# RWKV blocks of a transformer kernel: 128x128 block-diagonal matrices against compact 64x64 ones

## The chip, the cores and the metric

One core of a Trainium2 chip runs the whole program in one launch. The metric is device time in microseconds (us) of that launch; lower is better. The inputs are 512 tokens of width 1024 in float32, and the weights come from HBM as a stream of 857 blocks of 128x512.

## The reference, cut to what matters

The program is a chain of layers: a SwiGLU block, a mixing layer, a second SwiGLU, then pooling, dilated attention, sparse attention and convolution layers. Only the mixing layer is touched. Half of it is an RWKV-7 recurrence over 8 heads of width 64, the other half differential attention:

```python
def rwkv7_scan(r, w, k, v, a, b):     # state S: value x key, per head
    def step(S, inp):
        r_t, w_t, k_t, v_t, a_t, b_t = inp
        sa = einsum('bhij,bhj->bhi', S, a_t)
        S = S * w_t + sa[..., None] * b_t + v_t[..., None] * k_t
        y = einsum('bhij,bhj->bhi', S, r_t)
        return S, y
...
y = (y - mu) * rsqrt(var + GN_EPS)            # per token and head
y = y * gn_w + gn_b + sum(r * k * r_k) * v
return y * gate
```

The kernel computes the recurrence in chunks of 64 tokens. Inside a chunk the effect of `sa` on later tokens is a unit triangular 64x64 matrix, which has to be inverted per head and chunk; between chunks a 64x64 state per head is carried on.

## The kernel before, in words

**Matmuls.** Weights and activations of the large matmuls are split into a high and a low part, and each product is three matmuls of 128 columns of weights and 512 moving columns (`mm3`, lines 594 to 596). A generator (`gemm_fg`, `gemm_tg`) yields after such a product, so that other work can be put between them; I call this a work step. The blocks of the recurrence are plain float32 matmuls, which the chip runs as two instructions each (two passes); a transpose is one.

**The mixing layer** (`mix_heads`). The heads are handled in four pairs (`hp`), two heads of 64 on the 128 partitions. For each pair there is a projection (`proj`), a preparation (`prep`, `rwkv_pair`: decay, normalised keys, transposes of keys and values), and two units (`rwkv_unit`), one for each half of the tokens. A unit has four groups: 2 heads by 2 blocks of 128 tokens; a block holds two chunks, so its matrices are 128x128 with two 64x64 blocks on the diagonal and zeros elsewhere. These zeros are set once (`MEMSET`).

The steps of a unit, by the name of the PSUM tile they write:

- A (L1198): 16 matmuls of 64x64 weights and 128 moving columns, then eight masks on VectorE (L1205) into X1, X2
- T (L1212): transposes of Z
- W (L1220) and TW (L1228), at five levels m = 2 to 32: the inverse Z and its transpose T are merged from blocks of m to blocks of 2m. After each of the first four, Z is made from T by four transposes (L1233) and a copy on ScalarE. At 32 the line is L1237
- pta, akv, PQ (L1242, L1248, L1253), 128x128
- E (L1259), M (L1268) and G (L1273, L1274) for each chunk
- S (L1286): the state from chunk to chunk, two matmuls and one VectorE instruction each; the second half waits for the first (`"chain" in sh`)
- Y (L1297, L1298, L1301): the output, from X1, X2 and the state, summed in PSUM
- the norm, then yT and gate (L1319, L1324, L1325).

**The order.** `fill(steps, filler, n)` takes n steps of `filler` after each step of `steps`. Here `steps` are the two units taken in turn, and `filler` is `work`, a chain of projections, preparations, attention and output rows, with `PACE = 1.0`. The preparation of the first pair runs ahead of it without filler. A planner turns this order into one queue for each engine and may move an instruction ahead of another that isn't ready; the queues are then fixed and each runs in order. PSUM gives this stretch 2 banks for large matmuls, 3 (`aux`) for the units, 2 for preparation and attention, and 1 for the attention's output. The weight stream holds 4 raw and 7 split blocks of 512 columns.

Of the kernel before, what the change touches and what calls it, by code (L numbers as in the profile page):

```python
# [48 lines left out]
PACE = 1.0  # L49
LAG = 7  # L50
# [19 lines left out]
MEMSET = 8  # L70
# [252 lines left out]
def consts():  # L323
# [6 lines left out]
    c["mz0"] = f((i[None, :] == i[:, None] + 1) & (i[None, :] % 2 == 1))  # L330
    for m in (2, 4, 8, 16, 32):
        row, col = i[:, None], i[None, :]
        c[f"lv{m}"] = f((row // (2 * m) == col // (2 * m)) & (row % (2 * m) >= m) & (col % (2 * m) < m))
# [180 lines left out]
class Build:  # L514
# [464 lines left out]
    def mix_heads(self, u, yd, yr, pm, xd):  # L979
# [50 lines left out]
        def prep(hp):  # L1030

            yield from self.rwkv_pair(hp, pairs[hp], lor, lw, pm, c, sh[hp])
# [10 lines left out]

        self.after(MEMSET, lambda: [nc.gpsimd.memset(ub[:, :2048], 0.0) for ub in ubs])
# [21 lines left out]
        def units(half):  # L1066
            for _ in range(half * LAG):
                yield
            for hp in range(4):
                while not sh[hp]:  # L1070
                    yield
                yield from self.rwkv_unit(hp, half, sh[hp], sgd, pm, c, ubs[half])
                sh[hp]["done"] = sh[hp].get("done", 0) + 1
# [13 lines left out]
        for _ in prep(0):  # L1087
            pass

        def wait_for(hp):  # L1090
            while sh[hp].get("done", 0) < 2:
                yield

        work = chain(
            proj(1),
# [6 lines left out]
        fill(interleaved([units(0), units(1)]), work, PACE)  # L1102
# [4 lines left out]
    def rwkv_pair(self, hp, tiles, lor, lw, pr, c, sh):  # L1107
# [6 lines left out]
        gup = tile_("gup", (P, 2, P), 2)  # L1114
# [46 lines left out]
        for j, (nm, src) in enumerate((("bt", eb), ("kt", ec), ("vt", v))):  # L1161
            yield
            pt = self.faux(f"pt_{nm}{hp}")
            for b in range(4):
                nc.tensor.transpose(pt[:, b * P : (b + 1) * P], src[:, b * P : (b + 1) * P], self.ident)
            tok[nm] = tile_(nm, (P, 4, P))
            self.copy(j, tok[nm].rearrange("p a b -> p (a b)"), pt)
# [8 lines left out]
    def rwkv_unit(self, hp, half, sh, sgd, pr, c, ub):  # L1176
        gup = sh["gup"]
        ar, bt, kt, tok, bv, dc, st, yr = (sh[k] for k in ("ar", "bt", "kt", "tok", "bv", "dc", "st", "y"))
# [3 lines left out]
        id = f"{hp}_{half}"  # L1182
        tile_ = lambda tag, shape, bufs=2: pr.tile(list(shape), F32, tag=f"ru_{tag}", name=f"ru_{tag}{id}", bufs=bufs)
        g4 = lambda a, n: a.rearrange("p (g n) -> p g n", n=n)
        X1, X2 = g4(ub[:, :1024], 256), g4(ub[:, 1024:2048], 256)
        Tm, Z, RH, PQ = (g4(ub[:, a : a + 512], 128) for a in (2048, 2560, 3072, 3584))
        groups = [(g, 2 * half + g // 2, g % 2) for g in range(4)]
        tk = lambda p: slice(p * P, (p + 1) * P)
        hd = lambda h: slice(64 * h, 64 * h + 64)

        ck = lambda p, q: slice(p * P + 64 * q, p * P + 64 * q + 64)
        yield
        ps = [self.aux(f"A{id}_{h}") for h in range(2)]
        for j, src in enumerate((bt, kt)):
            for x in range(2):
                for g, p, h in groups:
                    q, a = h ^ x, 256 * j + P * (g // 2)
                    mm(ps[h][hd(q), a : a + P], src[hd(h), ck(p, q)], ar[hd(h), :, ck(p, q)], start=True, stop=True)  # L1198
        for j, X in enumerate((X1, X2)):
            for h in range(2):  # L1200
                for q in range(2):
                    src = ps[h][hd(q), 256 * j : 256 * j + 256].rearrange("p (g s n) -> p g s n", s=2, n=64)
                    dst = X[hd(q), h::2].rearrange("p g (s n) -> p g s n", s=2)[:, :, :, hd(q)]
                    m2 = c["m2"][hd(q)].rearrange("p (s n) -> p s n", s=2).unsqueeze(1).to_broadcast([64, 2, 2, 64])
                    V.tensor_tensor(dst, src, m2, op=ALU.mult)  # L1205

        V.tensor_tensor(Z, X1[:, :, :P], c["mz0"].unsqueeze(1).to_broadcast([P, 4, P]), op=ALU.mult)
        V.tensor_tensor(Z, Z, self.ident.unsqueeze(1).to_broadcast([P, 4, P]), op=ALU.add)
        yield
        ps = self.aux(f"T0{id}")  # L1210
        for g in range(4):
            nc.tensor.transpose(ps[:, tk(g)], Z[:, g], self.ident)  # L1212
        S.copy(Tm, g4(ps, P))
        W = RH
        halves = lambda a, m: a.rearrange("p g (b two m) -> p g two b m", two=2, m=m)
        for m in (2, 4, 8, 16, 32):
            yield
            ps = self.aux(f"W{id}_{m}")
            for g in range(4):
                mm(ps[:, tk(g)], X1[:, g, :P], Tm[:, g], start=True, stop=True)  # L1220
            V.tensor_tensor(W, g4(ps, P), c[f"lv{m}"].unsqueeze(1).to_broadcast([P, 4, P]), op=ALU.mult)
            yield
            ps = self.aux(f"TW{id}_{m}")
            out = ps.rearrange("p (x g b m) -> p x g b m", x=2, g=4, m=m)
            left, right = halves(Tm, m)[:, :, 0], halves(Z, m)[:, :, 1]
            if m < 32:
                for g in range(4):
                    mm(out[:, 0, g], Z[:, g], halves(W, m)[:, g, 0], start=True, stop=True)  # L1228
                V.tensor_tensor(left, left, out[:, 0], op=ALU.add)
                yield  # L1230
                ps = self.aux(f"Z{id}_{m}")
                for g in range(4):
                    nc.tensor.transpose(ps[:, tk(g)], Tm[:, g], self.ident)  # L1233
                S.copy(Z, g4(ps, P))
            else:
                for g in range(4):
                    mm(out[:, 1, g], W[:, g], right[:, g], start=True, stop=True)  # L1237
                V.tensor_tensor(right, right, out[:, 1], op=ALU.add)
        yield
        pa = self.aux(f"pta{id}", 256)  # L1240
        for q in range(2):
            nc.tensor.transpose(pa[:, tk(q)], ar[:, 0, tk(2 * half + q)], self.ident)  # L1242
        S.copy(RH[:, :, :64], g4(pa, 64))
        bt_, kt_, vt_ = tok["bt"], tok["kt"], tok["vt"]
        yield
        ps = self.aux(f"akv{id}", 256)
        for g, p, h in groups:
            mm(ps[:, g * 64 : (g + 1) * 64], X2[:, g, :P], vt_[:, p, hd(h)], start=True, stop=True)  # L1248
        S.copy(RH[:, :, 64:], g4(ps, 64))
        yield  # L1250
        ps = self.aux(f"PQ{id}")
        for g, p, h in groups:
            mm(ps[:, tk(g)], Z[:, g], RH[:, g], start=True, stop=True)  # L1253
        S.copy(PQ, g4(ps, P))

        yield
        ps = self.aux(f"E{id}", 256)
        for g, p, h in groups:
            mm(ps[hd(h), tk(g // 2)], PQ[:, g, :64], X1[:, g, P:], start=True, stop=True)  # L1259
        E = RH[:, :2].rearrange("p a b -> p (a b)")  # L1260
        V.tensor_tensor(E, ps, ar[:, 1, half * 256 : (half + 1) * 256], op=ALU.add)
        M = RH[:, 2:].rearrange("p a (q n) -> p a q n", q=2)
        Gs = Tm[:, :2].rearrange("p a (q n) -> p a q n", q=2)
        for q in range(2):
            yield
            ps = self.aux(f"M{id}_{q}", 128)
            for g, p, h in groups:
                mm(ps[hd(h), hd(g // 2)], PQ[hd(q), g, :64], bt_[hd(q), p, hd(h)], start=True, stop=True)  # L1268
            V.tensor_tensor(M[:, :, q], g4(ps, 64), c["i64"].unsqueeze(1).to_broadcast([P, 2, 64]), op=ALU.add)
            yield  # L1270
            ps = self.aux(f"G{id}_{q}", 128)
            for g, p, h in groups:
                mm(ps[hd(h), hd(g // 2)], bt_[hd(q), p, hd(h)], PQ[hd(q), g, 64:], start=True, stop=False)  # L1273
                mm(ps[hd(h), hd(g // 2)], kt_[hd(q), p, hd(h)], vt_[hd(q), p, hd(h)], start=False, stop=True)  # L1274
            dcq = dc[:, 4 * half + q : 4 * half + q + 3 : 2]
            V.tensor_tensor(Gs[:, :, q], g4(ps, 64), dcq.unsqueeze(2).to_broadcast([P, 2, 64]), op=ALU.mult)
        while half and "chain" not in sh:
            yield
        for cc in range(4):
            ch = 4 * half + cc  # L1280
            if ch == 7:
                break
            yield
            ps = self.aux(f"S{id}_{cc}", 64)
            for h in range(2):
                mm(ps[hd(h)], M[hd(h), cc // 2, cc % 2], st[hd(h), ch], start=True, stop=True)  # L1286
# [938 lines left out]
```

## Time and profile before

| | |
|---|---|
| median of 3 runs | 2875.74 us (2873.99 to 2876.14) |
| the profiled execution | 2876.86 us |
| its span, first to last instruction | 2875.0 us |
| TensorE matmul busy | 2816.1 us, 98% of the span |
| VectorE, ScalarE busy | 1544.8 us (54%), 1194.8 us (42%) |
| the units of the recurrence | from about 443 to 839 us |

PE is TensorE's matmul queue, PEld its weight loads, DVE VectorE, ACT ScalarE, POOL GpSimd, SP the queue that issues DMAs. A matmul's duration in a row runs to its modelled end, and the next one starts before that; what a matmul costs is read from start to start.

### The profile page before, as it was taken

The page shows a single profiled execution, that of the slowest core. Times are in us where ns is not written, and L with a number is a line of the kernel's source. Part 1 is how long each engine was busy: PE and PEld are TensorE (multiplying, and loading weights), DVE is VectorE, ACT ScalarE, POOL GpSimd, SP SyncE. Part 2 cuts the span into 40 slices and gives each one's busy share as a digit, 9 for nine tenths or more (in the row PEclk, how much of TensorE's full clock was granted, in tenths as well). Part 3 has the DMA queues.
Part 4 walks back from the last instruction along what each step waited for, and adds up shares of the span by engine and source line. Part 5 has one row for each costly group of instructions (what it writes and reads, how often), then busy time and mean ns, then how long its engine had stood idle before and what let it go on. Part 6 is the DMA issues. An engine that isn't in the chain of part 4 may idle for free.

```text
span 2875.0 us, 44121 instructions
## 1 busy us (share of the span) xinstructions
PE 2816.1 (98%) x16743; PEld 2390.0 (83%) x16743; DVE 1544.8 (54%) x3349; ACT 1194.8 (42%) x2504; POOL 430.6 (15%) x509
## 2 busy tenths in 40 slices
PE   8999999999999999999999999999999999999998
PEld 7888887868878888888888888889999787888887
DVE  5443276565666443255445533444566995577732
ACT  5333253233334333343333444444455646554431
POOL 2110041010014110011312200011004023200001
PEclk9999999999999999999999999999999999999999
DMA  4333351101122333333232332222232412133332
GB/s 142 96 99 96 99 164 37 41 21 41 34 71 79 100 96 96 103 96 96 88 107 81 89 104 78 89 84 76 77 93 81 107 59 67 61 104 97 96 95 74
DMA packets 136140, 245.30 MB, mean 85 GB/s; under 512 B 15064, under 2 KB 22232, under 8 KB 135800
## 3 DMA queue, kind: packets, MB, share of 16 engines
q1 hardware_dynamic: 135928, 242.49, 28.1%
q8 instruction: 131, 2.15, 0.3%
q14 instruction: 81, 0.66, 0.1%
HBM read 235.75 MB, written 6.68 MB: 84 GB/s over the span
## 4 chain that ended last, share of the span: by engine, by line
PE 87%; DVE 6%; ACT 2%; POOL 2%; issue 1%; DMA 1%; SPq 0%; POOLq 0%; DVEq 0%; ACTq 0%
PE f_gu L594 5%; PE f_gu L596 5%; PE f_gu L595 5%; PE kq L594 3%; PE kq L595 3%; PE kq L596 3%; PE cf L596 3%; PE cf L595 3%; PE cf L594 3%; PE f L594 3%; PE f L595 3%; PE f L596 3%; PE dO L1606 2%; PE v L594 2%; PE v L596 2%; PE v L595 2%
## 5 line engine op out<-in xcount | busy, mean ns | idle before, releaser
L184 DVE TENSOR_TENSOR wlo<-wraw,whi 128x512 fp32r<-128x512 f32 (+1 forms) x858 | 625.8, 734 | 698.7 <-ACT whi L183 697.3
L183 ACT CAST whi<-wraw 128x512 fp32r<-128x512 f32 (+1 forms) x858 | 528.4, 619 | 917.9 <-PE f_gu L596 275.0
L594 PE MATMUL f<-f_ah,wlo 128*128 128x512 f32 (+1 forms) x440 | 153.7, 349 | 1.1 <-DVE wlo L184 1.1
L596 PE MATMUL f<-f_ah,whi 128*128 128x512 f32 (+1 forms) x440 | 153.3, 348 | 0.0
L595 PE MATMUL f<-f_al,whi 128*128 128x512 f32 (+1 forms) x440 | 153.2, 348 | 0.0
L594 PE MATMUL f_gu<-n_uh,wlo 128*128 128x512 f32 (+1 forms) x376 | 142.8, 381 | 8.3 <-ACT n_uh L788 7.3
L594 PE MATMUL f_gu<-won_uh,wlo 128*128 128x512 f32 (+1 forms) x376 | 142.7, 379 | 0.0
L595 PE MATMUL f_gu<-n_ul,whi 128*128 128x512 f32 (+1 forms) x376 | 142.5, 379 | 0.0
L596 PE MATMUL f_gu<-won_uh,whi 128*128 128x512 f32 (+1 forms) x376 | 142.5, 379 | 0.0
L596 PE MATMUL f_gu<-n_uh,whi 128*128 128x512 f32 (+1 forms) x376 | 142.3, 379 | 0.0
L595 PE MATMUL f_gu<-won_ul,whi 128*128 128x512 f32 (+1 forms) x376 | 142.1, 378 | 0.0
L594 PE MATMUL cf<-w3on_uh,wlo 128*128 128x512 f32 (+1 forms) x376 | 141.5, 376 | 0.0
L595 PE MATMUL cf<-w3on_ul,whi 128*128 128x512 f32 (+1 forms) x376 | 141.2, 375 | 0.0
L596 PE MATMUL cf<-w3on_uh,whi 128*128 128x512 f32 (+1 forms) x376 | 141.1, 375 | 0.0
L594 PE MATMUL kq<-dl_uh,wlo 128*128 128x512 f32 x256 | 101.9, 398 | 0.0
L595 PE MATMUL kq<-dl_ul,whi 128*128 128x512 f32 x256 | 100.5, 393 | 0.0
L1576 ACT ACTIVATE ds<-ds,dmx 128x128 f32<-128x128 f32 (+1 forms) x192 | 79.7, 417 | 49.8 <-DVE dmx L1575 49.8
L596 PE MATMUL kq<-dl_uh,whi 128*128 128x512 f32 x256 | 99.8, 390 | 0.0
L594 PEld LDWEIGHTS f<-f_ah,wlo 128*128 128x128 f32 x440 | 82.6, 188 | 13.4 <-DVE wlo L184 1.3
L596 PEld LDWEIGHTS f<-f_ah,whi 128*128 128x128 f32 x440 | 82.6, 188 | 12.2
L595 PEld LDWEIGHTS f<-f_al,whi 128*128 128x128 f32 x440 | 82.6, 188 | 12.1
L594 PEld LDWEIGHTS f_gu<-n_uh,wlo 128*128 128x128 f32 x376 | 71.9, 192 | 21.3 <-ACT n_uh L788 7.3
(831 smaller groups left out, 7511.3 us busy)
## 6 DMA issues: line engine op xcount, KB each, us to landing
wraw<-w SPq DMA_DIRECT2D x856, 256.0 KB, 2.6
dperm<-dnat SPq DMA_DIRECT2D x4, 528.0 KB, 3.1
dl_acc<-dperm SPq DMA_DIRECT2D x4, 528.0 KB, 3.8
x<-x SPq DMA_DIRECT2D x4, 512.0 KB, 6.1
xd<-x SPq DMA_DIRECT2D x8, 256.0 KB, 2.9
x<-xd SPq DMA_DIRECT2D x8, 256.0 KB, 3.4
toep<-rvd SPq DMA_DIRECT2D x8, 256.0 KB, 4.7
out<-x SPq DMA_DIRECT2D x16, 128.0 KB, 1.8
```

The costliest lines, as they stand in the source:

```text
L183: b.nc.scalar.copy(hi[:, s], raw[:, s])
L184: b.nc.vector.tensor_tensor(lo[:, s], raw[:, s], hi[:, s].bitcast(F32), op=ALU.subtract)
L594: mm(ps, a[1], b[0], start=start, stop=False)
L595: mm(ps, a[0], b[1], start=False, stop=False)
L596: mm(ps, a[0], b[0], start=False, stop=stop)
L1576: S.activation(o, o, AF.Exp, bias=mx[:, i, h : h + 1], scale=-1.0, accum_out=zz[:, i, h : h + 1])
L1606: mm(po[0][:, i % 2, h], pT[:, b, a + j * P : a + (j + 1) * P], vt[:, kt, h * 64 : (h + 1) * 64], start=j == 0, stop=j == nb - 1)
```

## The change

Every block of the recurrence is stored as 64x64 on 64 partitions, chunk q of a block on partitions 64q to 64q+63, so that the 128x128 matrices with their zeros go. Both halves of the tokens are handled in one unit of eight groups (4 blocks by 2 heads). `rwkv_unit` becomes `rwkv_head` (A to G, and the part of Y that needs no state, `yl`) and `rwkv_tail` (the chain S, the part of Y from the state, norm, yT, gate). The tail of a pair is stepped beside the head of the next pair. Z is no longer made from T by transposes: both are updated by matmuls. `PACE` is 3, and the first preparation takes two steps of the next pair's projection after each of its own. `gup` and two of the transposed operands keep one buffer instead of two or lie in the units' memory, and the zeroing goes.

```diff
-PACE = 1.0
-LAG = 7
+PACE = 3
...
-        self.after(MEMSET, lambda: [nc.gpsimd.memset(ub[:, :2048], 0.0) for ub in ubs])
...
+        def units():
+            tail = iter(())
             for hp in range(4):
                 while not sh[hp]:
+                    next(tail, None)
                     yield
+                for _ in self.rwkv_head(hp, sh[hp], c, at):
+                    next(tail, None)
+                    yield
+                for _ in tail:
+                    yield
+                tail = self.rwkv_tail(hp, sh[hp], sgd, pm, c, at)
+            for _ in tail:
+                yield
...
-        for _ in prep(0):
-            pass
+        first = proj(1, apart("z1"))
+        fill(prep(0), first, FIRST_PACE)
...
-        fill(interleaved([units(0), units(1)]), work, PACE)
+        fill(units(), work, PACE)
...
-        gup = tile_("gup", (P, 2, P), 2)
+        gup = tile_("gup", (P, 2, P))
...
+        groups = [(2 * p + h, p, h) for p in range(4) for h in range(2)]
+        each = [(g, p, h, q) for g, p, h in groups for q in range(2)]
+        crossed = [(2 * p + h, p, h, h ^ x) for p in range(4) for x in range(2) for h in range(2)]
...
+            for g, p, h, q in crossed:                                  # A
+                mm(ps[h][hd(q), p * P : (p + 1) * P], src[hd(h), ck(p, q)], ar[hd(h), :, ck(p, q)], start=True, stop=True)
+            for h in range(2):
+                V.tensor_tensor(X[:, h::2], g4(ps[h]), c["m2"]..., op=ALU.mult)
...
+            for g, p, h, q in each:                                     # W
+                mm(ps[hd(q), blk(g)], X1[hd(q), g, :64], Tm[hd(q), g], start=True, stop=True)
+            V.tensor_tensor(W, g8(ps), bc(c[f"lv{m}"]), op=ALU.mult)
+            yield
...
+            for g, p, h, q in each if m < 32 else ():                   # TW
+                mm(out[hd(q), 0, g], Z[hd(q), g], halves(W, m)[hd(q), g, 0], start=True, stop=True)
+            for g, p, h, q in each:
+                mm(out[hd(q), 1, g], W[hd(q), g], right[hd(q), g], start=True, stop=True)
+            if m < 32:
+                V.tensor_tensor(left, left, out[:, 0], op=ALU.add)
+            V.tensor_tensor(right, right, out[:, 1], op=ALU.add)
...
+        for g, p, h, q in crossed:                                      # E, then M
+            mm(ps[q][hd(h), blk(p)], PQ[hd(q), g, :64], X1[hd(q), g, 64:], start=True, stop=True)
...
+        ps = self.aux(f"yl{hp}")
+        for g, p, h in groups:
+            for q in range(2):
+                mm(ps[hd(q), blk(g)], X1[hd(q), g, 64:], PQ[hd(q), g, 64:], start=True, stop=False)
+            for q in range(2):
+                mm(ps[hd(q), blk(g)], X2[hd(q), g, 64:], vt_[hd(q), p, hd(h)], start=False, stop=True)
...
+        for ch in range(1, 7):                                          # S, in rwkv_tail
             for h in range(2):
+                mm(ps[hd(h)], M[hd(h), ch], st[hd(h), ch], start=True, stop=True)
+            V.scalar_tensor_tensor(st[:, ch + 1], ps, dc[:, ch : ch + 1], Gs[:, ch], op0=ALU.mult, op1=ALU.add)
             yield
+        for ch in range(8):                                             # Y
+            p, q = ch // 2, ch % 2
+            for h in range(2):
+                mm(py[h][hd(q), 64 * p : 64 * p + 64], E[hd(h), ch], st[hd(h), ch], start=True, stop=True)
```

T (16 matmuls with the 64x64 identity), akv and PQ go over `each` as W does; PQ has 128 moving columns. G goes over `crossed`, two matmuls for each entry.

## Rows read from the trace of the kernel before

**Rows 1.** Busy time in stretches: us, each engine's busy us (instructions), clock, DMA

```profile
428.00:450.00 22.00, 20.95 (x125) 15.26 (x125) 16.37 (x31) 10.81 (x17) 5.29 (x3) 0.92 0.20 61
...
656.00:840.00 184.00, 181.67 (x1418) 145.22 (x1416) 110.64 (x292) 61.57 (x129) 11.32 (x11) 1.00 0.14 43
sum 390.00, PE 381.81 PEld 303.01 DVE 235.73 ACT 132.01 POOL 28.29; mean PE 127.27 PEld 101.00 DVE 78.58 ACT 44.00 POOL 9.43
```

**Rows 2.** Chain of waits, 560 to 571 us: start us, us, piece

```profile
562.92 0.23 PE rkv L596
563.14 0.84 PE TW L1228 x8
563.99 0.44 PE Z L1233 x4
...
565.64 1.79 PE W L1220 x16
```

**Rows 3.** PE in order of time, 511 to 518 us: start, us, engine line instruction

```profile
511.31 0.40 PE L596 MATMUL dqk<-f1n_uh,whi 128*128 128x512 f32 x1
511.64 0.33 PE L1286 MATMUL S<-rw_st,ub 64*64 64x64 f32 x4
511.90 0.50 PE L594 MATMUL dqk<-f1n_uh,wlo 128*128 128x512 f32 x1
512.24 0.39 PE L595 MATMUL dqk<-f1n_ul,whi 128*128 128x512 f32 x1
...
513.97 0.33 PE L1297 MATMUL Y<-ub 128*128 128x64 f32 x2
...
515.57 0.50 PE L594 MATMUL dqk<-f1n_uh,wlo 128*128 128x512 f32 x1
...
516.47 0.34 PE L1273 MATMUL G<-x,rw_bt 64*64 64x64 f32 x4
516.63 0.29 PE L1274 MATMUL G<-rw_vt,rw_kt 64*64 64x64 f32 x4
516.75 0.33 PE L1273 MATMUL G<-x,rw_bt 64*64 64x64 f32 x4
516.87 0.33 PE L1274 MATMUL G<-rw_vt,rw_kt 64*64 64x64 f32 x4
517.13 0.50 PE L594 MATMUL dqk<-f1n_uh,wlo 128*128 128x512 f32 x1
```

**Rows 4.** PE in order of time, around an M step at 493 us

```profile
493.34 0.45 PE L1268 MATMUL M<-rw_bt,ub 64*64 64x64 f32 x8
493.72 0.50 PE L594 MATMUL dqk<-f1n_uh,wlo 128*128 128x512 f32 x1
```

**Rows 5.** PE in order of time, an A step at 531 us

```profile
530.82 0.68 PE L1198 MATMUL A<-rw_ar,rw_eb 64*64 64x128 f32 x16
531.30 0.67 PE L1198 MATMUL A<-rw_ar,k 64*64 64x128 f32 x16
531.90 0.39 PE L594 MATMUL dv<-whi,f1n_ul 128*128 128x256 f32 x1
```

**Rows 6.** PE in order of time, an E step at 585 us

```profile
584.68 0.40 PE L596 MATMUL rkv<-f1n_uh,whi 128*128 128x512 f32 x1
585.00 0.66 PE L1259 MATMUL E<-ub 128*64 128x128 f32 x8
585.59 0.60 PE L474 MATMUL d_o<-dv,d_pT 128*128 128x128 f32 x3
```

**Rows 7.** Groups by line, 400 to 860 us: busy us, mean ns | idle before

```profile
L1221 DVE TENSOR_TENSOR x<-W,cst 128x512 f32<-128x512 f32 x20 | 13.8, 690 | 18.1 <-PE W L1220 17.9
```

**Rows 8.** Waits of the DMA queue, 450 to 840 us: us in total, times, longest

```profile
SPq L1115 <- PE gate L1325: 18.3, 2, 17.4
```

**Rows 9.** PE in order of time, an A step at 551 us beside an attention score

```profile
551.52 0.43 PE L1198 MATMUL A<-rw_ar,rw_eb 64*64 64x128 f32 x2
551.88 0.48 PE L441 MATMUL d_ps<-dqk 64*128 64x128 f32 x2
```

More of the change, by code (lines that the diff above doesn't have):

```diff
@@ L1030, in prep @@
         def prep(hp):
-            yield from self.rwkv_pair(hp, pairs[hp], lor, lw, pm, c, sh[hp])
+            yield from self.rwkv_pair(hp, pairs[hp], lor, lw, pm, c, sh[hp], ubs[0])
         diff = DiffAttention(self, u, yd, pm, c)
@@ L1085, in apart @@
             return zs
-        for _ in prep(0):
-            pass
+        first = proj(1, apart("z1"))
+        fill(prep(0), first, FIRST_PACE)
         def wait_for(hp):
-            while sh[hp].get("done", 0) < 2:
+            while "done" not in sh[hp]:
                 yield
         work = chain(
-            proj(1),
+            first,
             shared(diff.project(0), prep(1), PREP_PACE),
@@ L1174, in rwkv_pair, with rwkv_places @@
         sh.update(gup=gup, ar=ar, bt=eb, kt=ec, tok=tok, bv=v, dc=dc, st=st, y=r)
-    def rwkv_unit(self, hp, half, sh, sgd, pr, c, ub):
+    def rwkv_places(self, ub):
+        lo, hi = ub
+        g8 = lambda a: a.rearrange("p (g n) -> p g n", g=8)
+        t = dict(X1=g8(lo[:, :1024]), X2=g8(lo[:, 1024:2048]), PQ=g8(lo[:, 2048:3072]))
+        for j, n in enumerate(("T", "Z", "W", "E", "M", "G", "yl", "yc")):
+            t[n] = g8(hi[:, 512 * j : 512 * (j + 1)])
+        t["R"] = hi[:, :3072].rearrange("p (a n) -> p a n", a=2)[:, :, :512].rearrange("p a (g n) -> p a g n", g=8)
+        return t
@@ L1181, in rwkv_unit @@
         mm = nc.tensor.matmul
[L1182 to L1188, printed above, removed]
@@ L1207, in rwkv_unit @@
[L1207 to L1216, printed above, removed]
-            yield
[L1218 to L1284, printed above, removed]
-            for h in range(2):
-                mm(ps[hd(h)], M[hd(h), cc // 2, cc % 2], st[hd(h), ch], start=True, stop=True)
-            V.scalar_tensor_tensor(st[:, ch + 1], ps, dc[:, ch : ch + 1], Gs[:, cc // 2, cc % 2], op0=ALU.mult, op1=ALU.add)
-        yc = Tm[:, 2:].rearrange("p a (q n) -> p (a q) n", q=2)
@@ new lines, in rwkv_tail @@
+        py = [self.aux(f"Y{hp}_{h}", 256) for h in range(2)]
+        for ch in range(8):
+            p, q = ch // 2, ch % 2
+            for h in range(2):
+                mm(py[h][hd(q), 64 * p : 64 * p + 64], E[hd(h), ch], st[hd(h), ch], start=True, stop=True)
+        for h in range(2):
+            V.tensor_tensor(yc[:, h::2], py[h].rearrange("p (g n) -> p g n", g=4), yl[:, h::2], op=ALU.add)
+        s = tile_("s", (P, 8))
+        b8 = lambda a: a.unsqueeze(2).to_broadcast([P, 8, 64])
@@ L1315, in rwkv_unit @@
+        G.tensor_tensor(rd, v2, self.mhalf[:, :1].to_broadcast([P, 8]), op=ALU.pow)
+        V.tensor_tensor(yc, yc, b8(rd), op=ALU.mult)
         for _ in range(1 + NORM_WAIT):
             yield
-        pt = self.aux(f"yT{id}", 256)
-        for q in range(2):
-            nc.tensor.transpose(pt[:, tk(q)], yc[:, 2 * q : 2 * q + 2].rearrange("p a b -> p (a b)"), self.ident)
-        cs = slice(half * 256, (half + 1) * 256)
-        t1 = Z[:, 2:].rearrange("p a b -> p (a b)")
-        V.scalar_tensor_tensor(t1, pt, self.pv("gn_w", hp), bv[:, cs], op0=ALU.mult, op1=ALU.add)
@@ L1323, in rwkv_unit @@
-        pg = self.aux(f"gate{id}", 256)
-        mm(pg, gup[:, 0], sgd[:, 0, cs], start=True, stop=False)
-        mm(pg, gup[:32, 1], sgd[:32, 1, cs], start=False, stop=True)
-        V.scalar_tensor_tensor(yr[:, cs], t1, self.pv("gn_b", hp), pg, op0=ALU.add, op1=ALU.mult)
+        pt = self.aux(f"yT{hp}")
+        for p in range(4):
+            nc.tensor.transpose(pt[:, p * P : (p + 1) * P], yc[:, 2 * p : 2 * p + 2].rearrange("p a b -> p (a b)"), self.ident)
+        t1 = yl.rearrange("p a b -> p (a b)")
@@ L1329, in ln_residual @@
+        V.scalar_tensor_tensor(t1, pt, self.pv("gn_w", hp), bv, op0=ALU.mult, op1=ALU.add)
+        pg = self.aux(f"gate{hp}")
+        mm(pg, gup[:, 0], sgd[:, 0], start=True, stop=False)
+        mm(pg, gup[:32, 1], sgd[:32, 1], start=False, stop=True)
+        V.scalar_tensor_tensor(yr, t1, self.pv("gn_b", hp), pg, op0=ALU.add, op1=ALU.mult)
+        sh["done"] = True
     def ln_residual(self, src, kt, wname, l, name, rms_g=None, ls=2):
```

139 lines of the change are left out of this document (91 added, 48 removed).

## The prediction, made before the run

> **What bounds the kernel now.** I read the busy time by stretch first, then the chain of waits, then TensorE's queue in order of time. In the stretch of the units, 450 to 840 us, PE is busy 381.8 of 390 us at full clock, VectorE 235.7 and ScalarE 132.0 [rows 1]. The chain of waits there runs from matmul to matmul [rows 2]: what ends a stretch is how long TensorE's queue is, and the 8.2 us in which it stands idle. So I price the change in TensorE time from start to start, then ask whether the new chain of steps can stall the queue, and whether another engine comes up. VectorE's load falls: one mask of W for both halves instead of two of 0.69 us [rows 7], at five levels and four pairs, is 14 us less, and the masks of A go from 16 to 4 a pair. I put these at nothing; TensorE's queue hides them.
>
> **Prices.** A large product's matmul costs 0.23 us [rows 2]. A step with 128x128 weights costs 0.11 us for each instruction: 1.79 for 16 of W, 0.84 for 8 of TW (its moving columns are half, so the weights set the price), 0.44 for 4 transposes [rows 2]. These slip in between large matmuls at no further cost.
>
> A step on 64x64 tiles is different. Its two tiles take passes side by side: in G four instructions, two passes on each tile, start every 0.12 us, so a pass costs 0.06 on its tile [rows 3]. M with four passes a tile holds the queue 0.38 us [rows 4], so 0.14 is fixed. Its neighbours pay too: S starts 0.33 after the large matmul ahead of it instead of 0.23, and the large matmul behind it holds the queue 0.34 instead of 0.23 [rows 3]. A visit to 64x64 tiles thus costs 0.14 + 0.10 + 0.11 = 0.35 us plus 0.06 for each pass of the tile that has most. G with 8 passes checks it: 0.14 + 0.48 = 0.62, measured 0.66 [rows 3]. With 128 moving columns, A: 32 instructions on four tiles, 8 passes each, 1.08 us [rows 5], (1.08 - 0.14) / 8 = 0.118 a pass.
>
> **The change, for one pair, before to after.**
> - A: two visits of 8 passes on four tiles both times. Nothing.
> - T: 8 transposes, 0.88, to 16 matmuls, 16 passes on each of two tiles, 0.35 + 0.96 = 1.31. +0.43.
> - W: five levels of 1.79 (both halves) to 1.31. -2.40.
> - TW with Z at four levels: 16 instructions of TW, 1.79, and 8 transposes, 0.88, to 32 matmuls, 32 passes a tile, 0.35 + 1.92 = 2.27. -1.60. Level 32: 1.79 to 1.31, -0.48.
> - akv: 16 instructions with 128x128 weights, 1.79, to 1.31. -0.48. PQ: 1.79 to 0.35 + 16 x 0.118 = 2.24. +0.45. pta: the same four transposes.
> - E, M, G, Y, S before: E twice 0.59 + 0.20 [rows 6]; M four times 0.38 + 0.21; G four times 0.66 + 0.21; Y four times 1.60 + 0.11 [rows 3], because it mixes both shapes; S seven times 0.26 + 0.21. That is 1.58 + 2.36 + 3.48 + 6.84 + 3.29 = 17.55. After: E and M in one visit on four tiles, 16 passes, 1.31; G on four tiles (16 passes) and yl on two (32) in one visit, 0.35 + 2.88 = 3.23; Y's part from the state on four tiles, 8 passes, 0.83; six S, which for three pairs lie next to a step of the next head and cost 0.26 each, and for the last pair 0.47: 1.88 on average. Sum 7.25. -10.30.
> - gate and yT: the same columns, half the instructions. Nothing.
>
> Together 0.43 - 2.40 - 1.60 - 0.48 - 0.48 + 0.45 - 10.30 = -14.38, times four pairs -57.5 us. Two terms aren't shown by a row of before: four tiles at 64 moving columns, and two tiles over 16 or 32 passes in a row. At the dear end a pass costs the G visit's whole 0.66 less 0.14 over 8, 0.065: with some 340 passes a pair that takes back 1.7 us, 7 us in all. At the cheap end it costs half of the 0.11 of 128 columns of weights, 0.055, and gives 7 us more. If four tiles cost what two cost twice (E, M, G, Y: 40 passes), 2.4 a pair, 10 us. I keep 0.06 and both ends for the range.
>
> **What moves.** The steps of a pair are one chain now instead of two that take turns, with three work steps between, nine matmuls, 2.05 us. A step's answer needs its last passes to drain, about 0.3 (a piece of G lasts 0.29 to 0.34 though the next one starts after 0.12 [rows 3]), and VectorE's 0.69 [rows 7], some 1.0 to 1.1; with another VectorE instruction of the same size ahead of it 1.7 to 1.8. So 2.05 covers it. What waits behind a late step is the whole queue of TensorE. In attention the work steps are lighter than a product and the cover is thinner. Counting yields, the work has about 283 steps after the first preparation. Head 0 and 1 use it up to step 102; the third preparation ends at step 142, so for 40 steps there is no head beside projection and attention; heads 2 and 3 and the last tail need 43 steps of three, to 274. So the chain ends just before the work does, and its last output isn't waited for longer than now. The three `aux` banks now serve a head and a tail; A and E/M take two banks each, G and yl all three, so a bank can be late by one VectorE instruction, 0.69. Stalls: the idle time of 8.2 us could go (-8), or 25 of the 77 head and tail steps could lack 1 us each (+25). I take +3, near the row, since the queue is planned in the same way.
>
> The first preparation gets the next pair's projection as filler. The planner has put such matmuls there already: PE is busy 20.95 of 22 us, at clock 0.92 [rows 1]. From 0 to -2; I take -1. The single `gup` makes its load wait for the gate of the pair just before; with two buffers it waited up to 17.4 us for a gate already [rows 8], and behind it on SP stand weight loads, with up to seven split blocks, 2.7 us of matmuls each, ahead. Nothing, or up to 5 us if blocks run out. Zeroing leaves POOL, 28.3 of 390 us busy [rows 1]: nothing.
>
> Sum against the profiled execution, 2876.9: -57.5 + 3 - 1 = -55.5, 2821.4. The median of the runs shown is 1.1 lower, so 2820.
>
> **Rivals.**
> 1. The two tiles of a diagonal pair don't run side by side. T, W, TW, akv and yl lie on tiles (rows 0 to 63, outputs 0 to 63) and (64 to 127, 64 to 127) and write one PSUM bank, and M and G, from which the price of a pass comes, use two tiles with the same rows. If such a pair took turns, passes double: 16 + 80 + 144 + 16 + 32 = 288 x 0.06 = 17.3, and PQ 16 x 0.118 = 1.9, 19.2 a pair, 77 us: 2897, slower. It turns the sign when 72% of that is lost (55.5 of 77). Against it: S before is just such a pair in one bank, and its four instructions hold the queue 0.26 us [rows 3]; side by side my price says 0.14 + 2 x 0.06 = 0.26, in turn 0.38. But S has two passes, not 32. The Trainium skill, TensorEngine Tiling (Array Packing), section Restrictions and Gotchas, says that different row tiles can't use one PSUM bank at the same time and that software has to see to it; by that rule the result would be this rival's, and the row on S speaks against it here.
> 2. The single chain is exposed: half of the 77 steps find their operand about 1 us late, in the attention stretches above all, +38: 2858. For it: one chain, three banks. Against: 2.05 us of cover and PE idle 8.2 us of 390 now.
> 3. Visits are broken up. The planner moves instructions: an A step before is split by an attention score after two instructions [rows 9]. If each of 77 visits is split once, 77 x 0.35 = +27: 2847.
> 4. The tail doesn't run beside the next head: pairs wait for their preparation, and the tail of the second pair runs alone. That is six visits with their own 0.21, 1.3 us a pair: it changes little, and lies inside the likeliest range.
>
> **How the numbers follow.** Likeliest, gain as priced: 65%, 2820, its own range 2798 to 2840 (pass price 7 either way, four tiles 10, stalls -8 to +10). Rivals 2 and 3: 20%, 2840 to 2866. Rival 1: 8%. A larger gain, below 2798, where stalls go and passes are cheaper: 7%. The range 2795 to 2855 leaves out rival 1, most of the larger gain and the upper part of 2 and 3. A measurement of this kernel can tell about 0.2%, 5.8 us. Faster by more: all but rival 1 and a corner of rival 2, 0.88; within: 0.02; slower: 0.10.
>
> **What would show it.** Right: W's 32 instructions start over about 1.0 us, TW's 64 over 2.0; the passes of two tiles start in pairs; the large matmuls have the same count; PE stays over 95% busy between the first unit and the output projection, and that stretch is 55 us shorter; VectorE is less busy. Wrong: W over 2 us (rival 1), PE idle before W or TW with VectorE as releaser (rival 2), many short pieces of W or TW between large matmuls (rival 3).

## The result and the profile after

The changed kernel takes 2810.53 us (median of 4 runs, 2809.79 to 2813.22), the kernel before 2874.94 beside it (2873.99 to 2876.14): a ratio of 0.9777, 95% interval 0.9761 to 0.9794. The forecast was 2820, in a range of 2795 to 2855. The profiled execution took 2810.96 us, its span is 2809.2.

The page's head shows VectorE 42 us less busy than before, and TensorE still 98% busy:

```profile
span 2809.2 us, 46679 instructions
...
PE 2746.5 (98%) x18151; PEld 2329.2 (83%) x18151; DVE 1502.6 (53%) x3209; ACT 1172.5 (42%) x2454; POOL 424.3 (15%) x503
```

Busy time in stretches, with the columns of [rows 1]. The last unit's step now starts at 760 us instead of 838, and PE keeps 97% of the stretch:

```profile
428.00:450.00 22.00, 20.93 (x152) 14.64 (x150) 16.66 (x29) 13.06 (x21) 4.65 (x3) 0.92 0.19 61
450.00:771.00 321.00, 310.64 (x4383) 240.64 (x4383) 192.47 (x473) 106.57 (x215) 26.11 (x21) 0.99 0.15 47
```

The chain of waits after, where [rows 2] had W at 1.79, TW at 0.84 and Z at 0.44 for one unit. It is still TensorE's queue from matmul to matmul, with one W for both units' work:

```profile
528.50 0.23 PE rkv L595
528.73 1.08 PE W L1236 x32
529.81 0.12 PE S L1311 x4
...
532.39 1.05 PE TW L1243 x32
533.44 0.58 PE TW L1245 x19
```

PE in order of time after. W's 32 instructions hold the queue 0.98 and 1.08 us (to the next start), TW's 64 from 524.21 to 526.10, 1.89; a step of the previous pair's chain, S, lies right behind and shares the visit. The large matmul behind W at 537.01 holds 0.33 instead of 0.23, as [rows 3] had it:

```profile
520.67 1.15 PE L1236 MATMUL W<-x,ub 64*64 64x64 f32 x32
521.65 0.28 PE L1311 MATMUL S<-rw_st,x 64*64 64x64 f32 x4
521.86 0.39 PE L593 MATMUL dv<-whi,f1n_ul 128*128 128x256 f32 x1
...
524.21 1.12 PE L1243 MATMUL TW<-x 64*64 64x32 f32 x32
525.16 1.10 PE L1245 MATMUL TW<-x 64*64 64x32 f32 x32
526.10 0.31 PE L1311 MATMUL S<-rw_st,x 64*64 64x64 f32 x4
...
537.01 1.15 PE L1236 MATMUL W<-x,ub 64*64 64x64 f32 x32
538.09 0.50 PE L593 MATMUL rkv<-f1n_uh,wlo 128*128 128x512 f32 x1
538.42 0.39 PE L594 MATMUL rkv<-f1n_ul,whi 128*128 128x512 f32 x1
```

And a visit on four tiles, E and M together, which [rows 4] and [rows 6] had in six pieces a pair: 64 instructions from 564.58 to 565.67.

```profile
564.58 0.69 PE L1271 MATMUL EM<-ub 64*64 64x64 f32 x32
565.09 0.65 PE L1273 MATMUL EM<-ub 64*64 64x64 f32 x32
565.67 0.59 PE L440 MATMUL d_ps<-dqk 64*128 64x384 f32 x2
```

VectorE's mask of W, as long as in [rows 7]. These 20 are all of them now; of the kernel before, [rows 7] shows one unit's 20, and the other unit had as many in a group of its own.

```profile
L1237 DVE TENSOR_TENSOR x<-W,cst 128x512 f32<-128x512 f32 x20 | 13.8, 690 | 19.3 <-PE W L1236 19.3
```

**Where the time went.** I summed TensorE's time from start to start, by the tile written, from the first matmul of the first preparation to the last one ahead of the output projection: 411.2 us before, 340.6 after, -70.6.

| | before | after |
|---|---|---|
| steps of the recurrence | 182.9 | 119.6 |
| attention | 34.2 | 30.2 |
| preparation | 24.7 | 21.8 |
| large matmuls (685 in both) | 160.7 | 158.7 |
| idle | 8.7 | 10.3 |

The whole execution gained 65.8 by its span, so some 5 us were lost again elsewhere. Behind the stretch, from the first matmul of the output projection on, the changed kernel takes 2038.1 us instead of 2034.3; times the granted clock there, 0.9916 and 0.9934, both are 2021, so these 3.7 us went to the clock. The other 1.1 lie ahead of the stretch, where TensorE stands idle 2.4 us longer and loses 1.7 us less to the clock. Over the whole span the mean clock is 0.994 before and 0.992 after. As far as TensorE sets the pace, span times clock gives the same execution in us at full clock (1.00, the 2.4 GHz level): 2857.8 and 2786.7, a difference of 71.1, close to the gain of the stretch. One of the after kernel's spells at 0.50 (1.2 GHz) is the first 6 us of the output projection:

```profile
771.00:777.00 6.00, 5.92 (x26) 5.70 (x27) 4.22 (x8) 3.57 (x8) 0.00 (x0) 0.50 0.32 89
777.00:787.00 10.00, 10.00 (x85) 10.00 (x84) 3.46 (x8) 2.93 (x7) 4.59 (x7) 0.98 0.17 54
```

That product of span and clock is used below beside the times. The clock is given to 0.001, so a product is good to about 1.4 us; a median over a kernel's runs stands in the table.

| kernel | time, us | ratio to before, 95% | span x clock, us |
|---|---|---|---|
| before | 2874.9 to 2876.9 | | 2859 |
| after | 2810.53 | 0.9777 (0.9761 to 0.9794) | 2786 |
| e1_in_turn | 2889.97 | 1.0029 (1.0005 to 1.0054) | 2829 |
| e2_w_two_banks | 2806.78 | 0.9760 (0.9743 to 0.9776) | 2790 |
| e3_split_visits | 2819.11 | 0.9802 (0.9788 to 0.9817) | 2801 |
| e4_tail_after | 2816.38 | 0.9795 (0.9780 to 0.9810) | 2799 |
| e5_z_transposed | 2819.97 | 0.9802 (0.9788 to 0.9817) | 2795 |
| e6_prep_alone | 2805.78 | 0.9757 (0.9742 to 0.9772) | 2788 |
| e7_pace1 | 2826.53 | 0.9828 (0.9813 to 0.9843) | 2810 |
| e8_quarters32 | 2797.47 | 0.9731 (0.9715 to 0.9747) | 2779 |
| e9_q32_prep | 2806.83 | 0.9757 (0.9743 to 0.9772) | 2779 |
| e10_q32_split | 2803.39 | 0.9745 (0.9728 to 0.9761) | 2779 |

### The profile page after: what moved, and what is told of

Its sections match the earlier page's. It is cut to its first block, busy times and chain, and to the rows that moved or that the text cites. A ratio compares the mean times of both kernels' runs of the same rounds, so it can differ in the third digit from the quotient of the medians.

```text
span 2809.2 us, 46679 instructions
## 1 busy us (share of the span) xinstructions
PE 2746.5 (98%) x18151; PEld 2329.2 (83%) x18151; DVE 1502.6 (53%) x3209; ACT 1172.5 (42%) x2454; POOL 424.3 (15%) x503
## 4 chain that ended last, share of the span: by engine, by line
PE 86%; DVE 6%; ACT 2%; POOL 2%; issue 2%; DMA 1%; SPq 0%; POOLq 0%; DVEq 0%; ACTq 0%
PE f_gu L593 6%; PE f_gu L595 6%; PE f_gu L594 5%; PE kq L593 3%; PE kq L594 3%; PE kq L595 3%; PE cf L593 3%; PE cf L594 3%; PE cf L595 3%; PE f L593 3%; PE f L594 3%; PE f L595 3%; PE dO L1625 2%; PE v L593 2%; PE v L594 2%; PE v L595 2%
## 5 line engine op out<-in xcount | busy, mean ns | idle before, releaser
L593 PEld LDWEIGHTS f<-f_ah,wlo 128*128 128x128 f32 x440 | 82.6, 188 | 13.4 <-DVE wlo L183 1.3
```

The source lines that it names most:

```text
L593: mm(ps, a[1], b[0], start=start, stop=False)
```

## The experiments

**e1_in_turn: the two tiles of a diagonal pair one after the other.** The same matmuls, all on one tile first, then all on the other.

```diff
-        each = [(g, p, h, q) for g, p, h in groups for q in range(2)]
+        each = [(g, p, h, q) for q in range(2) for g, p, h in groups]
...
-            for g, p, h, q in each[8 * a : 8 * a + 8]:
+            for g, p, h, q in [e for e in each if e[0] // 4 == a]:
```

> The changed kernel with one edit: the list `each` goes over all blocks on the first diagonal tile and then over all on the second, so T, W, TW, akv and PQ have the same matmuls in another order. Theory A (two tiles take passes side by side only because neighbouring matmuls in the queue are on different tiles; starts are in order): each group of 32 instructions takes 0.93 us more (16 x 0.058), W about 2.0 us instead of 1.08; 16 such groups and PQ (1.7) a pair, 16.6 us a pair, 66 in all: 2877 us, as before the change. Rival (each tile has its own queue, so order doesn't matter): W stays 1.08 us and the time 2811.

Measured: 2889.97 us in the median, 0.3% above the kernel before. PE in order of time, a W and a TW step: W holds the queue from 455.39 to 457.21, 1.82 us instead of 1.08; TW from 460.06 to 463.28, 3.22 instead of 1.89.

```profile
455.39 1.90 PE L1236 MATMUL W<-x,ub 64*64 64x64 f32 x32
457.21 0.50 PE L593 MATMUL rkv<-f1n_uh,wlo 128*128 128x512 f32 x1
...
460.06 1.67 PE L1243 MATMUL TW<-x 64*64 64x32 f32 x29
...
461.71 1.65 PE L1245 MATMUL TW<-x 64*64 64x32 f32 x29
463.28 1.05 PE L1134 MATMUL pn<-cst,rw_di 128*128 128x2 f32 x8
```

So without passes side by side the gain by time is gone, and they are had only where neighbours in the queue lie on different tiles. The Trainium skill, TensorE: Matmul & The Clock Gate, section Step-by-step: what each phase is for, says that matmuls stay in program order and only weight loads are pulled ahead; this trace agrees, with 1.08 against 1.82 us for the same 32 instructions. A pass in turn costs (1.82 - 0.14) / 16 = 0.105 us, side by side (1.08 - 0.14) / 16 = 0.059: somewhat less than the double that rival 1 assumed.

By span times clock this order costs 43 us, some 60% of the gain and less than the 66 that were forecast (W came to 1.82 us, not 2.0); by time it costs 79, and the rest is the clock. The windows show the clock fall right behind the TW at 470 us, though PE was busy all the time (0.50 from 472.85 us on, 0.61 on average in the first row), and the mean over 450 to 600 us is 0.89 (after: 1.00):

```profile
472.00:476.00 4.00, 4.00 (x24) 3.28 (x21) 3.08 (x6) 0.00 (x0) 1.19 (x1) 0.61 0.00 0
476.00:482.00 6.00, 6.00 (x85) 5.17 (x84) 2.63 (x4) 1.21 (x2) 0.00 (x0) 0.98 0.16 46
```

Its ten runs lie between 2869.5 us (mean clock 0.987) and 2899.1 (0.975); their products all lie between 2825 and 2831.

**e2_w_two_banks: W's two tiles in a PSUM bank each.**

```diff
-            ps = self.aux(f"W{hp}_{m}")
+            pw = [self.aux(f"W{hp}_{m}_{q}") for q in range(2)]
             for g, p, h, q in each:
-                mm(ps[hd(q), blk(g)], X1[hd(q), g, :64], Tm[hd(q), g], start=True, stop=True)
-            V.tensor_tensor(W, g8(ps), bc(c[f"lv{m}"]), op=ALU.mult)
+                mm(pw[q][hd(q), blk(g)], X1[hd(q), g, :64], Tm[hd(q), g], start=True, stop=True)
+            for q in range(2):
+                V.tensor_tensor(W[hd(q)], g8(pw[q])[hd(q)], c[f"lv{m}"][hd(q)]..., op=ALU.mult)
```

> The changed kernel, but W's two diagonal tiles write two PSUM banks, each taken out by a VectorE instruction on 64 partitions. Theory A (different row tiles on different partitions of one bank don't hinder each other): W's 32 instructions still take 1.08 us; the time is 2811 to 2820, the excess from 20 more VectorE instructions of about 0.7 us on the chain. Rival (the rule that row tiles can't share a bank costs something here): W gets shorter, towards 0.6 us, and up to 10 us are gained in TensorE time.

Measured: 2806.78 us, 3.7 less, but by span times clock 3.5 more: no gain that the work shows. The group of W's matmuls, over the stretch to the output projection, in this kernel and then in the changed one (busy us, mean ns):

```profile
L1236 PE MATMUL W<-x,ub 64*64 64x64 f32 x640 | 23.5, 221 | 0.0
```

```profile
L1236 PE MATMUL W<-x,ub 64*64 64x64 f32 x640 | 23.3, 221 | 0.6 <-DVE x L1247 0.5
```

Summed from start to start, W took 21.7 us in two banks and 21.5 in one: sharing the bank costs nothing here. The rule of the Trainium skill, TensorEngine Tiling (Array Packing), section Restrictions and Gotchas, that different row tiles can't use one bank at the same time, isn't borne out for these two tiles, which write different partitions of it.

**e3_split_visits: each W and TW in two steps.** `PACE` goes to 2 so that the work lasts as long.

```diff
-            for g, p, h, q in each:
+            for i, (g, p, h, q) in enumerate(each):
+                if i == 8:
+                    yield
                 mm(ps[hd(q), blk(g)], X1[hd(q), g, :64], Tm[hd(q), g], start=True, stop=True)
...
```

> The changed kernel with the steps W and TW cut in two, each half its own step (two work steps between, PACE 2 instead of 3, so that the filler for a pair stays the same): 40 more visits to 64x64 tiles, the same passes. Theory A (a visit costs 0.35 us beside its passes, in itself and at its neighbours): +14 us, 2824. Rival (only passes cost): 2811 within 4.

Measured: 2819.11 us; the stretch to the output projection is 352.1 us instead of 340.6, +11.5: recurrence +6.0, large matmuls +4.9. A piece of W is half as long now:

```profile
523.57 0.68 PE L1238 MATMUL W<-x,ub 64*64 64x64 f32 x16
524.09 0.28 PE L1315 MATMUL S<-rw_st,x 64*64 64x64 f32 x4
```

The planner joined some of the pieces again: the changes in the queue between 128x128 and a smaller tile rise from 201 to 255, which is 27 more visits instead of 40, (6.0 + 4.9) / 27 = 0.40 us each, against 0.35 in the prediction. Nearly half of it lies on the large matmuls, as priced there.

**e4_tail_after: the tail of a pair behind its head, not beside the next one.** `PACE` is 2.4.

```diff
-                for _ in self.rwkv_head(hp, sh[hp], c, at):
-                    next(tail, None)
-                    yield
-                for _ in tail:
-                    yield
-                tail = self.rwkv_tail(hp, sh[hp], sgd, pm, c, at)
-            for _ in tail:
-                yield
+                yield from self.rwkv_head(hp, sh[hp], c, at)
+                yield from self.rwkv_tail(hp, sh[hp], sgd, pm, c, at)
```

> The changed kernel, but each pair's tail follows its head instead of running beside the next head (PACE 2.4, so that the longer chain uses up the work at the same place). Theory A (TensorE's queue is the bound, and a tail step beside a head step only shares the fixed cost of a visit): 18 S visits and 3 Y visits get their own 0.21 us, +4 to 5: 2815. Rival (the overlap is what lets the chain end in time): idle time of TensorE grows, 2825 or more.

Measured: 2816.38 us, the stretch 8.1 us longer (recurrence +2.8, large matmuls +2, idle 13.7 instead of 10.3). PE's waits name the norm's transposes, yT, 4.8 us in four waits against 2.3 in two in the changed kernel. Running the tail beside the next head, with the `PACE` that goes with it, is worth some 6 us by time and 12 by span times clock, of the 72.

```profile
PE yT L1332 <- DVE x L1327: 4.8, 4, 1.5
```

**e5_z_transposed: Z from T by transposes again,** on the compact blocks.

```diff
-            for g, p, h, q in each:
-                mm(out[hd(q), 1, g], W[hd(q), g], right[hd(q), g], start=True, stop=True)
             if m < 32:
                 V.tensor_tensor(left, left, out[:, 0], op=ALU.add)
-            V.tensor_tensor(right, right, out[:, 1], op=ALU.add)
+                yield
+                ps = self.aux(f"Z{hp}_{m}")
+                for g, p, h, q in each:
+                    mm(ps[hd(q), blk(g)], Tm[hd(q), g], c["i64"][hd(q)], start=True, stop=True)
+                S.copy(Z, g8(ps))
...
```

> The changed kernel, but at levels 2 to 16 Z is made again from T, now by 16 compact matmuls with the identity in a step of their own and a ScalarE copy, instead of its own update. Same number of passes, 16 more visits. Theory A (passes and visits are what costs): 16 x 0.35 = +6, and a chain of 16 more steps that outlasts the work by some steps, up to +4: 2816 to 2821. Rival (the update of Z without a transpose is itself a large part of the gain): +14 or more, as much as the transposes cost before.

Measured: 2819.97 us; TW and Z together 38.2 us of the queue instead of 35.5, the stretch +9.5. The new matmuls cost what the old ones cost; what is added is 16 visits and idle time, 13.9 instead of 10.3, with the longest wait where the last norm comes late:

```profile
PE yT L1344 <- DVE x L1339: 8.4, 3, 6.8
```

**e6_prep_alone: the first preparation without filler.**

```diff
-        fill(prep(0), first, FIRST_PACE)
+        for _ in prep(0):
+            pass
```

> The changed kernel, but the first preparation is traced without the next pair's projection as filler, as before the change. Theory A (the planner puts these matmuls there by itself): within 2 us of 2811. Rival (the filler of the first preparation is part of the gain): +4 or more, with idle time of TensorE between 428 and 450 us.

Measured: 2805.78 us, 4.7 less, a time that neither theory had; the output projection starts 1.7 us later, and by span times clock there is no difference (2788 against 2786). The filler is worth nothing that can be told; what this build wins is clock.

**e7_pace1: one work step between two steps of the chain.**

```diff
-PACE = 3
+PACE = 1
```

> The changed kernel with one work step instead of three after each step of the chain. One work step covers 0.69 us, a step's answer needs 1.0 to 1.1 and more behind other VectorE work. Theory A (the cover is what keeps TensorE from waiting): some 0.4 us late on each of 77 steps, +20 to +40, 2830 to 2850, with idle time ahead of W and TW released by VectorE. Rival (the planner moves large matmuls up by itself): 2811 within 5.

Measured: 2826.53 us, below the theory's range, the stretch +20.2: idle 16.0 instead of 10.3, recurrence +7.5, large matmuls +4.8, preparation +3.5. The theory's sign is missing too: PE's waits show none ahead of W or TW, and the longest in total is for yT, 5.3 us. The last gate is done at 737 us in a stretch that ends at 791, so the chain runs out early and attention then has no cover. The pace matters, but most of the 20 us are not waits; that the planner keeps the steps of the chain covered by moving large matmuls up fits this and is not shown by itself.

**e8_quarters32: the merges up to level 16 on 32x32 tiles.** A 64x64 triangle below level 32 has only its two 32x32 blocks on the diagonal; here T, W and TW of levels 2 to 16 lie on four diagonal tiles of 32x32, and level 32 is as it was. (T and Z are widened to 64 columns before it, by two instructions each on ScalarE and VectorE.)

```diff
-        for m in (2, 4, 8, 16, 32):
+        quarters = [(g, j) for g in range(8) for j in range(4)]
+        for m in (2, 4, 8, 16):
...
+            for g, j in quarters:
+                mm(ps[qt(j), 32 * g : 32 * g + 32], X1[qt(j), g, qc(j)], Tc[qt(j), g], start=True, stop=True)
...
+            for g, j in quarters:
+                mm(out[qt(j), 0, g], Zc[qt(j), g], halves(Wc, m)[qt(j), g, 0], start=True, stop=True)
+            for g, j in quarters:
+                mm(out[qt(j), 1, g], Wc[qt(j), g], right[qt(j), g], start=True, stop=True)
```

> A further step: up to level 16 the merges need only the 32x32 blocks on the diagonal, so T, W and TW at levels 2 to 16 are done on four 32x32 tiles with 32 columns of weights. The same number of passes on each tile, but each with half the columns. Theory A (a pass costs what its weights' columns cost, 0.058 us for 64, so 0.03 for 32): T and W 0.46 less, TW 0.93 less, 6 us a pair, 24 in all: 2787 to 2792. Rival 1 (starts on four tiles come no faster than the 15 ns that E and M show): no change, 2811. Rival 2 (a quarter of the array at work lets the clock fall, as with passes in turn): clock below 0.95 in the stretch and 2811 or more.

Measured: 2797.47 us, the fastest of all, 13.1 less than the changed kernel by time and 7.5 by span times clock. W's 64 instructions hold the queue 0.69 us, against 1.08 for 32 on 64x64 tiles; the recurrence takes 101.6 us instead of 119.6, -18 of the 24 that were forecast. Of these, 8 go back in idle time, 18.3 instead of 10.3, so that the time misses 2787 to 2792; a part of the idle time lies inside a run of small matmuls, where the profile names no releaser ("issue"). PE in order of time:

```profile
471.78 0.40 PE L595 MATMUL dqk<-f1n_uh,whi 128*128 128x512 f32 x1
472.11 0.43 PE L1250 MATMUL TW<-x 32*32 32x16 f32 x29
473.31 0.46 PE L1250 MATMUL TW<-x 32*32 32x16 f32 x34 [0.78 <-issue]
...
517.92 0.75 PE L1243 MATMUL W<-x,ub 32*32 32x32 f32 x64
518.61 0.33 PE L1333 MATMUL S<-rw_st,x 64*64 64x64 f32 x4
```

**e9_q32_prep: e8 with e6's lone preparation.** The diff is e6's.

> The quarters of e8 with the first preparation run alone, as in e6. e6 was 4.7 us faster than the changed kernel although its mixing layer took 1.6 us more: what it won lay behind the layer, where the changed kernel spends 2038.1 us and e6, e8 and the kernel before 2033.8 to 2034.3. Theory: that is the granted clock's spells at half speed behind the layer, which happen to differ from build to build and which e8 hasn't; then there is nothing left to win here, and the missing filler costs 1 to 3 us: 2797 to 2800. Rival: a lone first preparation is worth 4.7 us by itself (its filler takes the large matmuls away that later cover steps): 2792 to 2793, with the layer shorter than in e8.

Measured: 2806.83 us, 9.4 more than e8: both theories missed the time. By span times clock it is e8 (2779 and 2779), so there is nothing to win in the work, as the first theory had it; but that theory put the slow spells behind the mixing layer, and here most of them lie in it: in the profiled executions they cost 12.0 us there instead of 1.7 in e8, and 17.8 instead of 13.3 behind it. The mean clocks:

```profile
core 0: 2793.2 us, clock 0.995
```

```profile
core 0: 2809.2 us, clock 0.989
```

(e8, then this kernel.) In this kernel TW at 454 us stops for 1.34 us with no releaser, and then the clock is 0.50 for 10 us; a second such spell runs from 705 to 718 us, behind a gap of 0.97 us of the same kind:

```profile
454.35 0.46 PE L1253 MATMUL TW<-x 32*32 32x16 f32 x34
456.15 0.61 PE L1253 MATMUL TW<-x 32*32 32x16 f32 x28 [1.34 <-issue]
456.70 0.80 PE L595 MATMUL rkv<-f1n_uh,whi 128*128 128x512 f32 x1
```

```profile
452.00:456.00 4.00, 2.81 (x169) 2.06 (x168) 1.56 (x3) 0.62 (x1) 0.00 (x0) 1.00 0.19 72
456.00:466.00 10.00, 9.85 (x294) 7.05 (x293) 1.82 (x6) 0.00 (x0) 0.00 (x0) 0.50 0.10 30
```

**e10_q32_split: e8 with the two halves of TW in steps of their own.**

```diff
                 mm(out[qt(j), 0, g], Zc[qt(j), g], halves(Wc, m)[qt(j), g, 0], start=True, stop=True)
+            yield
             for g, j in quarters:
```

> The quarters of e8 with the two halves of TW (64 matmuls each) in steps of their own, so that three work steps lie between them. e8 has 8 us more idle time than the changed kernel, in gaps of 0.4 to 0.95 us inside runs of 64 small matmuls for which the profile names no releaser. Theory (the queue runs out of instructions in long runs of short ones): runs of 128 go, idle time falls from 18.3 to about 11 us, and 16 more visits at 0.35 to 0.4 us cost 6: 2795 to 2798, about as e8, with idle time moved into visits. Rival (the gaps are waits for operands that the profile doesn't show): idle time stays at 18 or grows, since W's answer has no more time than before, and the visits come on top: 2803 to 2806.

Measured: 2803.39 us, in the rival's range, but not for the rival's reason: the waits without a releaser are nearly gone. PE's waits without a releaser from 430 to 760 us, in e8 (2.5 + 1.3 + 0.8 = 4.6 us) and then in this kernel (0.3):

```profile
PE W L1243 <- issue: 2.5, 3, 0.9
...
PE TW L1252 <- issue: 1.3, 2, 0.8
...
PE TW L1250 <- issue: 0.8, 1, 0.8
```

```profile
PE TW L1253 <- issue: 0.3, 1, 0.3
```

So these gaps come with long runs of short instructions and go when the runs are halved. The traces also show what they wait for. Counted along TensorE's stream of matmuls and weight loads, all 16 such gaps of e8, e9 and e10 (7, 8 and 1) lie at the same place modulo 256, 193 or 194, and each ends 2.2 to 2.7 us after a load of 16 KB began on the DMA queue for instructions. For the gap of e8 that ends at 473.31 us that load began at 470.89; this is the queue's one load between 470.5 and 474.5 us:

```profile
q8 instruction: 1, 0.02, 1.4%
```

In the changed kernel 256 instructions take 4.3 us or more, and no gap of this kind is seen in the stretch; in e8 they take as little as 2.2. The gaps are waits for the next instructions. Even so, idle time falls only from 18.3 to 15.2 us, not to 11, since other waits grow (for yT 7.0 us instead of 2.3). The visits take the gain back: by span times clock the kernel equals e8, and by time it is slower by its clock, 0.991 to 0.993 against 0.991 to 0.995.

## Why the prediction was right

The result, 2810.53, lies in the range, 9.5 below the forecast, and the mechanism is the one predicted: a visit to 64x64 tiles at a fixed price, and passes side by side. That it lies so close is in part luck: the stretch gained 15 us more than forecast, and 5 were lost outside it. The terms in us, over four pairs, without the neighbours' share of a visit (0.21, a line of its own), against the sums by tile, rounded:

| step | predicted | measured |
|---|---|---|
| A | 0 | -4.2 |
| T | +0.9 | +0.6 |
| W | -13.8 | -15.2 |
| TW with Z | -12.5 | -13.4 |
| akv, PQ, pta | -1.8 | -0.9 |
| E, M, G, Y, S | -29.0 | -29.4 |
| gate, yT | 0 | -0.9 |
| large matmuls behind and ahead of visits | -1.3 | -2.0 |
| attention | not priced | -4.0 |
| preparation | -1 | -3.0 |
| stalls | +3 | +1.6 |
| sum of the stretch | -55.5 | -70.6 |
| the rest of the program | 0 | about +5 |

- **The price of a pass held** where no row of before showed it: 0.14 + 16 x 0.06 = 1.10 was forecast for W, 1.08 measured; 1.10 for E and M on four tiles, 1.09 measured (4.37 over four pairs); 3.02 for G with yl, 3.02 measured (12.07 over four). So neither of the two unknown terms, four tiles and long runs, had a price of its own. The largest single part is Y: with `yl` it went from 26.1 to 10.5 us.
- **W, TW and Z** gained 2.3 us more than priced. W cost 36.65 us before, 1.83 a step instead of the 1.79 of [rows 2], and 21.50 after, 1.08 instead of 1.10. TW with Z cost 48.87 before, 1.0 less than priced, and 35.48 after, 1.9 less than priced: 32 passes in a row held the queue 1.89 us, not 2.06.
- **The neighbours** came out near their price for another reason than given. The prediction let steps with 128x128 weights slip in "at no further cost". But in the kernel before, a large matmul right behind such a step holds the queue 0.32 us, too (0.315 in the median of 63), against 0.336 behind a 64x64 step. What belongs to the change of shape is the 0.10 ahead (0.326 in the median ahead of a 64x64 step, 0.233 ahead of one of 128x128):

```profile
474.16 0.60 PE L1233 MATMUL Z<-ident,ub 128*128 128x128 f32 x4
474.52 0.48 PE L594 MATMUL dqk<-f1n_uh,wlo 128*128 128x512 f32 x1
474.84 0.39 PE L595 MATMUL dqk<-f1n_ul,whi 128*128 128x512 f32 x1
```

- **A and attention were mis-sized.** I gave A nothing, with [rows 5]; but that step, 1.08 us, is the only one of eight that lay whole in the queue. The others lay in pieces, with preparation, attention's scores or other steps between, and took 1.4 to 1.9 each, 13.45 in all (after: 9.28, five of the eight whole at 0.92 to 1.03). Attention's scores took 16.39 us before and 13.24 after. Four of their instructions belong together, two on rows 0 to 63 and two on rows 64 to 127, and a piece with two of them holds the queue as long as one with all four: 0.41 us from 551.88 in [rows 9] to the next start, and 0.42 after. That is passes side by side once more. Before, 14 of 23 pieces had only two, after, 2 of 17. The first row is of before, the others of after:

```profile
552.29 0.35 PE L1198 MATMUL A<-rw_ar,rw_eb 64*64 64x128 f32 x4
```

```profile
698.95 0.49 PE L440 MATMUL d_ps<-dqk 64*128 64x128 f32 x4
699.37 0.83 PE L1243 MATMUL TW<-x 64*64 64x32 f32 x22
```

[Rows 9] stood in the prediction for a rival and was not priced as something that could go away. The changes of shape in the queue fell from 275 to 201, where the 1.3 us given to neighbours stand for 6 visits, 12 changes. Why fewer steps were broken up isn't shown; A wasn't changed alone.
- **Stalls**: idle time rose by 1.6, inside the +3. The cover of three work steps holds. With one (e7) the stretch takes 20.2 us more, but only 5.7 of that is idle time, and none of it is waits ahead of W or TW.
- **Rival 1** is what e1 measures: had the two tiles taken turns, the change would have been no gain, 2890 us. That this is near the rival's 2897 is luck: in work the turns cost 43 us, not 77, and the clock, which the rival didn't have, took the rest. The condition wasn't the bank (e2) but the order in the queue: `each` has q innermost, and I took the side-by-side price without asking what in the code gives it.
- **Rival 3** has its price from e3, 0.40 us a visit; after the change fewer visits were broken up, not more. **Rival 2** didn't come: the waits for VectorE ahead of W and TW sum to some 0.5 us. **Rival 4** was said to change little, 1.3 us a pair; e4 lost 6 to 12 us, of which 3.4 is idle time that came with the visits.
- **The rest of the program** I took as unchanged. Behind the stretch its work is, but the granted clock took 3.7 us back, and 1.1 came ahead of the stretch. Without that the result would have lain some 14 below the forecast, not 9.5: A and attention too small by 8, W and TW by 2, preparation and stalls by 3 make most of it.

## What to carry to other kernels

Price a small-tile step as a fixed charge for the visit plus the passes of the fullest tile, read both from start to start, and put matmuls of different tiles next to each other in the queue: that order alone decided between 2810 and 2890 us, 43 of them as work and the rest as clock. When steps get shorter, look also at what they used to break up: instructions that could run side by side may have been parted. When two builds differ by under 0.5%, multiply span by mean granted clock before explaining the difference: e6, e9 and e10 moved by 5 to 9 us in time and not in work.

## What the runs showed of the hardware that was not expected

- Two diagonal 64x64 tiles in one bank ran as fast as in two: 21.5 against 21.7 us of the queue for the 640 instructions of W. A pass on a 64x64 tile costs 0.059 us with a neighbour on the other tile and 0.105 without. On 32x32 tiles 64 instructions, 16 on each of four tiles, held the queue 0.69 us, (0.69 - 0.14) / 16 = 0.034 a pass.
- The granted clock fell to 0.50 with PE busy throughout, when one tile of the array was used at a time in T, W and TW (e1, 0.89 on average over 150 us), and behind gaps of 1.34 and 0.97 us (e9). A gap doesn't always bring it: in the changed kernel, 2.5 us without a matmul before 819.24 us were followed by full clock. What decides isn't settled by these runs.
- Runs of 64 and 128 instructions of about 0.01 us each stop for 0.2 to 1.3 us without a releaser, always at the same place modulo 256 in TensorE's stream and 2.2 to 2.7 us after a 16 KB instruction load began (e8, e9, e10). The Trainium skill, Runtime: NRT & Kernel Launch, section Instruction fetch mechanics, says that crossing a block of instructions is mostly hidden. In the changed kernel it is, with no such gap in the stretch; in e8 it isn't, 4.6 us.
